# A decoder trunk with three kinds of heads: four VectorE edits and another order of projections, index scores and search

## The chip, the cores and the metric

The kernel runs on one core of one Trainium2 chip. The metric is the device time of one execution in microseconds (us), as the median of the runs.

## The reference, cut to what matters

One layer for 1024 positions of width 1024, all in float32: a combined input projection, three groups of heads, a SiLU gate, an output projection and norms.

```python
h = x
u = rms_norm(h, attn_norm)
proj = einsum('bsd,dc->bsc', u, w_in)
(dq, dk, dv, sq, ckv, iq, ik, iw, rq, rk, rv, gate) = split(proj)

# group A: differential attention, 6 heads of two softmaxes each, causal
p = softmax(where(causal, einsum('bqhcd,bkhcd->bhcqk', qb, k) * scale, NEG))
a = p[:, :, 0] - lam * p[:, :, 1]
o_a = rms_norm(einsum('bhqk,bkhd->bqhd', a, v), diff_norm) * (1 - lam_init)

# group B: DSA, 6 heads; an indexer of 8 heads picks 256 keys for each query
rel = relu(einsum('bqhd,bsd->bqhs', iqb, ik))
score = einsum('bqhs,bqh->bqs', rel, iwb) * IDX_SCALE
_, sel = top_k(where(causal, score, NEG), 256)
# softmax over the selected keys of the latent c_kv, then up-projection

# group C: 4 heads of chunkwise retention with rotary q and k

mixed = concatenate([o_a, o_b, o_c], -1)
y = silu(gate) * mixed
out = rms_norm(h + einsum('bsc,cd->bsd', y, w_out), final_norm)
```

## The kernel before

Every float32 product of a projection is made of three TensorE products of a high and a low part of the operands (`mm3`, L130 to L132: high by high, high by low, low by high). A projection *unit* (q0, k0, g0, iq2 and so on) is 128 columns of the input projection: two halves of 512 positions with 24 matmuls each, into a PSUM tile `pG`, of which there are two. Weights come by DMA and are split on GpSimd (L119, L123). The g units are the gate: their eviction `gate_evac` takes exp(-x), Ln(1 + .), exp(-.) on ScalarE (L818, L820, L821), copies x from PSUM on ScalarE (L113, called through `cp`) and multiplies on VectorE (L822).

The stages, in the order of the program:

- The norm of x and its transposition (`prep_a`, `prep_b`).
- The index scores (`idx_scores`): for each of 8 heads (two for each of the units iq0 to iq3) and the query blocks 7 to 2, matmuls into a score tile `pS` (L342, L343), a relu on ScalarE (L345) and a multiply-add on VectorE (L350). A projection unit's result goes to DRAM and comes back in another layout (`stack`, tiles `st`) before scores can use it. In this block the order on TensorE is the order of the program text (`manual_schedule`): `interleave` mixes streams, each piece of work that a stream yields having a cost, and a stream's weight saying what share of the time it gets.
- One big `interleave` of three streams: `diff` for three pairs of heads (weight `wd` 36), the top-k search `topk` (weight `wt` 13), and most remaining projection units (weight `wg` 119). Here a list scheduler fixes each engine's order when the program is built, on the costs it assumes.
- DSA for the first half of the queries beside retention and the first output projection, then the second half with the other output projections.

`diff` has 48 softmax pairs (6 heads by 8 query blocks). For each, TensorE makes two score tiles (L649, `pS`, two buffers), VectorE adds the mask and takes the row's extreme (L660, which frees the score tile), ScalarE takes the exponential and the row sum (L662), and then `comb`: two reciprocals (L674, L676), a scaling of the first softmax on GpSimd (L675), the lambda multiplication of a 128x1 column (L677) and a multiply-add (L678). TensorE then transposes (L609) and multiplies by v (L624).

`topk` finds for each query the 256th largest index score bit by bit: 31 bits, in each of which VectorE counts for three blocks (L377) and ScalarE for three (L391), followed by three tiny VectorE operations (L396, L397, L398). After the last bit, the *ties* (L418 to L428) turn scores and threshold into an additive mask `bias` for each of the blocks 7, 6, 5, 4, 3 and 2, which DSA needs: a sign on ScalarE and seven VectorE operations.

Of the kernel before, what the change touches and what calls it, by code (L numbers as in the profile page):

```python
# [2 lines left out]

# [1 line left out]

# [23 lines left out]
    0, 384, 768, 1152, 1536, 1664, 2176, 2248, 2504, 2760, 3016)  # L29
WA = 384 + 72  # L30
C_R = (C_RQ, C_RK, C_RV)
K = {'mk': 'up ky', 'mp': 's2 g5 g4', 'rt': ('hl', 'pq'), 's0': ('gg', 'gg', 'ag', 'gg', 'vg', 'gg', 'vg', 'vg'), 'xp': 2, 'bufs': (8, 3, 3, 5, 3, 4, 1), 'pp': (7,), 'rot': 0, 'order': 'g0 g1 k1 q1 k2', 'order2': 'q2 g2 rq g6 s0 ck g7 s1 M g3 rv rk | ', 'wd': 36, 'wt': 13, 'wg': 119, 'gw': 56, 'rw': 26, 'rx': 132, 'pw': 40, 'ow': 84, 'nf': 2, 'ev': 200, 'late': 8, 'de': ('aa', 'aa', 'aa'), 'da': 'ax', 'gd': (7, 4, 2), 'hlp': 'sqkk', 'tkp': '', 'vt': 'v', 'rs': 'x', 'nv': 1, 'dn': 'v', 'gy': 'a', 'gm': 'v', 'ws': 'gg', 'oe': ('av', 'gg'), 'one': 0, 'idx': (42, 40), 'iqs': 'iq2 iq3 q0 k0'}
NST, NP, NPQ, NW, NHL, NHALF, NY = K["bufs"]


# [22 lines left out]
def interleave(*streams):  # L58
    for _ in mix(*streams):
        pass  # L60
# [8 lines left out]
class Trunk:  # L69
# [238 lines left out]
    def stack(self, key, g, order, c0=0, c1=S):  # L308
        n, _, r, _ = self.qd[key].shape
        q = self.slot("st", [128, S], FR)  # L310
# [45 lines left out]
    def topk(self):  # L356
        nc = self.nc
        gd = K["gd"]
        ga = tuple(b for b in range(7, 1, -1) if b not in gd)
        nv = {b: 128 * (b + 1) for b in range(2, NB)}  # L360
        sc = self.sc
        jv = self.const("jv", [128, 1024], BF)
        ja = self.const("ja", [128, 1024], mybir.dt.int8)
        hb = self.const("hb", [128, 1024], BF)
        nc.gpsimd.tensor_scalar(hb, sc[7].bitcast(BF)[:, 1::2], 1.0, 0.0, op0=OP.mult, op1=OP.add)
        cols = {b: j for j, b in enumerate(gd + ga)}
        nd_, nc_ = len(gd), len(cols)
        thr = self.const("thr", [128, nc_])
        for b, j in cols.items():
            nc.vector.memset(thr[:, j:j + 1], nv[b] - TOPK + 0.5 if b in gd else float(nv[b] - 2 * TOPK + 1))  # L370
        c = self.const("tk_c", [128, nc_], I32)
        m = self.const("tk_m", [128, nc_], I32)
        cnt = self.const("tk_n", [128, nc_])

        def count(b, t, op, bit=0):
            j = cols[b]
            nc.vector.tensor_scalar(jv[:, :nv[b]], hb if b == 7 and bit >= 16 else sc[b], t, 0.0, op0=op, op1=OP.add,  # L377
                                    accum_out=cnt[:, j:j + 1])

        def cut(b):  # L380
            return c[:, cols[b]:cols[b] + 1].bitcast(F)

        for b in gd + ga:
            count(b, 0.0, OP.is_ge)
            yield 0.8
        nc.vector.tensor_scalar(m, cnt, float(TOPK), -1.0, op0=OP.is_lt, op1=OP.mult)
        nc.vector.tensor_scalar(c, m, 1 << 30, None, op0=OP.bitwise_xor)
        for bit in range(30, -1, -1):
# [12 lines left out]
        for b in ga:  # L401
            count(b, cut(b), OP.is_gt)
        cf = c[:, nd_:].bitcast(F)
        nc.vector.scalar_tensor_tensor(w[:, 0], cf, -1.0, cf, op0=OP.mult, op1=OP.max)
        nc.vector.tensor_scalar(w[:, 1], cnt[:, nd_:], float(TOPK), 2.0 ** -24 * (1 + 2.0 ** -10), op0=OP.is_ge,
                                op1=OP.mult)
        nc.vector.tensor_tensor(w[:, 0], w[:, 0], w[:, 1], OP.mult)
        nc.vector.tensor_tensor(cf, cf, w[:, 0], OP.add)
        yield 2.4
        A, C, T3 = (self.sct[b].bitcast(BF) for b in (7, 5, 3))  # L410
        self.bias = {0: self.cb[:, 896:], 1: self.cb[:, 768:], 7: A[:, :1024], 6: A[:, 1024:1920], 5: C[:, :768],
                     4: C[:, 768:1408], 2: C[:, 1408:1792], 3: T3[:, :512]}
        for b in (7, 6, 5, 4, 3, 2):
            n, T = nv[b], cut(b)
            bias = self.bias[b]
            sg, eq, pre = jv[:, :n], hb[:, :n], sc[b]
            nd = self.sb.tile([128, 1], F, name=self.name("nd"), tag="nd", bufs=2)
            nc.scalar.activation(sg, sc[b], AF.Sign, bias=T, scale=-1.0, accum_out=nd)  # L418
            (nc.gpsimd if "e" in K["tkp"] else nc.vector).tensor_scalar(eq, sg, 0.0, 1.0, op0=OP.is_equal, op1=OP.mult)
            nc.vector.tensor_tensor_scan(pre, eq, eq, 0.0, OP.add, OP.bypass)  # L420
            nc.vector.tensor_tensor(nd, nd, pre[:, n - 1:n], OP.add)
            nc.vector.tensor_scalar(nd, nd, 0.5, TOPK - n / 2.0, op0=OP.mult, op1=OP.add)
            nc.vector.scalar_tensor_tensor(eq, pre, nd, eq, op0=OP.is_gt, op1=OP.mult)
            nc.vector.tensor_tensor(eq, eq, sg, OP.max)
            if "a" in K["tkp"]:
                nc.scalar.activation(bias, eq, AF.Copy, scale=NEG)
            else:
                (nc.gpsimd if "b" in K["tkp"] else nc.vector).tensor_scalar(bias, eq, NEG, 0.0, op0=OP.mult, op1=OP.add)  # L428
            yield n / 1024 * 5

    def pair(self, tag, bufs):
# [198 lines left out]
    def diff(self, pair):  # L630
# [35 lines left out]
        def comb(v):  # L666
# [6 lines left out]
            else:  # L673
                nc.vector.reciprocal(mx[:, 2:3], mx[:, 2:3])  # L674
                nc.gpsimd.tensor_scalar(P[0], P[0], mx[:, 2:3], 1.0, op0=OP.mult, op1=OP.mult)  # L675
                nc.vector.reciprocal(mx[:, 3:4], mx[:, 3:4])  # L676
                nc.vector.tensor_tensor(mx[:, 3:4], mx[:, 3:4], self.nlam, OP.mult)  # L677
                nc.vector.scalar_tensor_tensor(P[1], P[1], mx[:, 3:4], P[0], op0=OP.mult, op1=OP.add)  # L678
            return P[1]

# [18 lines left out]
    def dsa(self, pair, half):  # L699
        nc = self.nc  # L700

        def head(a):
            e = half * 512 + 512
            return [self.stack(f"sq{pair}", a, "hl", e - 512, e)] + [self.stack(f"kk{pair}", a, o, 0, e)
                                                                     for o in ("hl", "lh")]

        def scores(st, i):
            q2, kh, kl = st
# [100 lines left out]
    def gate_evac(self, c):  # L809
        nc = self.nc  # L810
        if c < 6:
            self.gd[c] = self.dram(f"gd{c}", [128, S])
        d = self.gd[c]

        def evac(half, ps):
            t = self.sb.tile([128, 2, 512], F, name=self.name("gt"), tag="hl", bufs=NHL)
            e, y = t[:, 0], t[:, 1]
            nc.scalar.activation(e, ps, AF.Exp, scale=-1.0)  # L818
            self.cp(K["gy"], y, ps)
            nc.scalar.activation(e, e, AF.Ln, bias=1.0)  # L820
            nc.scalar.activation(e, e, AF.Exp, scale=-1.0)  # L821
            (nc.gpsimd if K["gm"] == "g" else nc.vector).tensor_tensor(y, y, e, OP.mult)  # L822
            nc.sync.dma_start(d[:, half * 512:half * 512 + 512], y)
        return evac

    def run(self):
# [148 lines left out]
```

## Time and profile before

| what | value |
|---|---|
| median of 3 runs (lowest, highest) | 783.7 us (782.78, 785.11) |
| the profiled execution, its span | 781.83 us, 780.1 us |
| granted TensorE clock, mean over the span | 0.983 |
| TensorE matmul, busy | 720.0 us, 92% |
| VectorE, busy | 562.0 us, 72% |
| ScalarE, busy | 452.6 us, 58% |
| GpSimd, busy | 314.5 us, 40% |

The span is what the trace covers; the execution's own time is 1.7 us longer. Busy times are sums over instructions of one profiled execution. Two instructions that follow each other on TensorE overlap in the trace, so its busy share is no measure of how close it is to its peak.

### The profile page before, as it was taken

How to read it: one execution, taken by the hardware profiler on the slowest of the kernel's cores; microseconds unless marked ns; L12 is line 12 of the kernel's file. 1: busy time of each engine (PE TensorE's matmuls, PEld its weight loads, DVE VectorE, ACT ScalarE, POOL GpSimd, SP SyncE). 2: the span in 40 equal slices, each digit the busy share in tenths (PEclk: the TensorE clock that was granted, in tenths of full speed). 3: DMA queues.
4: the chain of work that ended last, by engine and by line, in shares of the span. 5: the costliest groups of instructions: out<-in, count | busy, mean ns of one | idle time of the engine just before them, and what ended most of it. 6: DMA issues, size and time to landing. Idle time of an engine off the chain costs nothing.

```text
span 780.1 us, 12935 instructions
## 1 busy us (share of the span) xinstructions
PE 720.0 (92%) x4314; PEld 590.4 (76%) x4314; DVE 562.0 (72%) x1319; ACT 452.6 (58%) x1004; POOL 314.5 (40%) x343
## 2 busy tenths in 40 slices
PE   3899999999999999979998879998978999999996
PEld 3798888888877898756876667897856777787884
DVE  5920277789999999989999999425676776664443
ACT  4521255559788876887855756532465666554332
POOL 6402323324415358437656788325732432120000
PEclk9999999999999999989999999999998999999998
DMA  9303645454375263361276385346579864313351
GB/s 333 79 1 81 189 137 158 133 140 116 105 183 149 71 176 95 107 158 47 66 202 183 115 241 151 114 162 212 162 228 277 272 204 119 117 48 109 119 176 59
DMA packets 93250, 113.05 MB, mean 145 GB/s; under 512 B 11904, under 2 KB 63488, under 8 KB 93056
## 3 DMA queue, kind: packets, MB, share of 16 engines
q1 hardware_dynamic: 91888, 109.61, 48.8%
q10 hardware_dynamic: 1296, 2.62, 0.9%
q8 instruction: 34, 0.56, 0.3%
q14 instruction: 32, 0.26, 0.1%
HBM read 75.50 MB, written 36.18 MB: 143 GB/s over the span
## 4 chain that ended last, share of the span: by engine, by line
PE 56%; DVE 23%; DMA 9%; issue 5%; ACT 4%; POOL 2%; SPq 1%; DVEq 0%; ACTq 0%; POOLq 0%
PE pG L130 5%; PE pG L131 5%; PE pG L132 5%; PE pB L624 5%; PE pB L609 4%; PE pG L283 4%; PE pG L282 4%; PE pG L931 4%; PE pG L284 4%; PE pG L932 4%; PE pG L930 4%; DVE jv L377 3%; DVE pp L678 2%; PE pS L343 2%; DMA wr<-in_w_in_dram 2%
## 5 line engine op out<-in xcount | busy, mean ns | idle before, releaser
L130 PE MATMUL pG<-uh,wh 128*128 128x512 f32 x352 | 141.6, 402 | 0.8 <-DVE vt L117 0.5
L132 PE MATMUL pG<-uh,wl 128*128 128x512 f32 x352 | 139.5, 396 | 0.0
L131 PE MATMUL pG<-ul,wh 128*128 128x512 f32 x352 | 139.4, 396 | 0.0
L123 POOL TENSOR_TENSOR wl<-wr,wh 128x512 fp32r<-128x512 f32 x56 | 79.7, 1439 | 110.9 <-PE pG L131 58.7
L391 ACT ACTIVATE ja<-sc,tk_c 128x896 int8<-128x896 f32 (+2 forms) x93 | 83.3, 896 | 19.9 <-DVE tk_c L398 12.6
L113 ACT ACTIVATE pt<-pB 128x512 f32<-128x512 f32 (+2 forms) x120 | 58.6, 496 | 41.2 <-PE pB L609 41.1
L609 PE MATMUL pB<-ident,pp 128*128 128x128 f32 x432 | 72.7, 286 | 9.1 <-ACT pt L113 2.1
L130 PEld LDWEIGHTS pG<-uh,wh 128*128 128x128 f32 x352 | 66.4, 189 | 15.0 <-issue 1.3
L132 PEld LDWEIGHTS pG<-uh,wl 128*128 128x128 f32 x352 | 66.3, 188 | 14.9
L131 PEld LDWEIGHTS pG<-ul,wh 128*128 128x128 f32 x352 | 66.4, 188 | 13.6 <-issue 0.7
L609 PEld LDWEIGHTS pB<-ident,pp 128*128 128x128 f32 x432 | 50.4, 143 | 25.8 <-issue 8.9
L377 DVE TENSOR_SCALAR_CACHE_REDUCE jv<-sc,tk_c 128x640 bf16<-128x640 f32 (+4 forms) x81 | 69.1, 853 | 0.7
L624 PE MATMUL pB<-pt,v 128*64 128x128 f32 x864 | 66.1, 288 | 2.7 <-ACT pt L113 2.0
L675 POOL TENSOR_SCALAR pq<-pq,mx 128x896 f32<-128x896 f32 (+7 forms) x48 | 41.4, 864 | 61.3 <-DVE mx L674 48.5
L119 POOL TENSOR_SCALAR wh<-wr 128x512 fp32r<-128x512 f32 x56 | 41.5, 745 | 60.5 <-DMA wr<-in_w_in_dram 58.4
L624 PEld LDWEIGHTS pB<-pt,v 128*64 128x64 f32 x864 | 53.7, 140 | 15.0 <-issue 6.1
L649 PE MATMUL pS<-st,st 128*128 128x512 f32 (+3 forms) x144 | 44.8, 373 | 13.3 <-DVE mx L660 10.6
L283 PE MATMUL pG<-wl,uh 128*128 128x256 f32 x192 | 55.0, 287 | 2.1 <-POOL wl L123 2.1
L282 PE MATMUL pG<-wh,uh 128*128 128x256 f32 x192 | 54.7, 287 | 2.1 <-POOL wh L119 1.0
L345 ACT ACTIVATE pp<-pS 128x1024 f32<-128x1024 f32 (+5 forms) x48 | 36.5, 760 | 31.2 <-PE pS L343 31.1
L350 DVE SCALAR_TENSOR_TENSOR sc<-pp,iw,sc 128x1024 f32<-128x1024 f32 (+5 forms) x42 | 43.6, 1045 | 14.7 <-ACT pp L345 14.0
L284 PE MATMUL pG<-wh,ul 128*128 128x256 f32 x192 | 53.8, 282 | 0.0
(220 smaller groups left out, 1772.1 us busy)
## 6 DMA issues: line engine op xcount, KB each, us to landing
wr<-in_w_in_dram SPq DMA_DIRECT2D x56, 256.0 KB, 3.1
st<-qdq SPq DMA_DIRECT2D x24, 256.0 KB, 4.3
st<-qkk SPq DMA_DIRECT2D x18, 256.0 KB, 6.2
x<-in_x_dram SPq DMA_DIRECT2D x8, 512.0 KB, 6.6
qiq<-hl SPq DMA_DIRECT2D x16, 256.0 KB, 3.5
st<-qiq SPq DMA_DIRECT2D x8, 512.0 KB, 3.4
wr<-in_w_out_dram SPq DMA_DIRECT2D x16, 256.0 KB, 4.3
xr<-in_x_dram SPq DMA_DIRECT2D x8, 512.0 KB, 3.6
```

The lines of the kernel that those rows point to most:

```text
L113: self.nc.scalar.activation(out, in_, AF.Copy)
L123: (self.nc.vector if e2 == "v" else self.nc.gpsimd).tensor_tensor(lo, src, hi.bitcast(F), OP.subtract)
L130: mm(ps, wh, xh, start=start, stop=False)
L131: mm(ps, wh, xl, start=False, stop=False)
L132: mm(ps, wl, xh, start=False, stop=stop)
L282: mm(ps, uh, hs[k], start=k == 0, stop=False)
L283: mm(ps, uh, ls[k], start=False, stop=False)
L284: mm(ps, ul, hs[k], start=False, stop=k == KC - 1)
L377: nc.vector.tensor_scalar(jv[:, :nv[b]], hb if b == 7 and bit >= 16 else sc[b], t, 0.0, op0=op, op1=OP.add, accum_out=cnt[:, j:j + 1])
L391: nc.scalar.activation(ja[:, :nv[b]], sc[b], AF.Sign, bias=cut(b), scale=-1.0, accum_out=cnt[:, cols[b]:cols[b] + 1])
L609: nc.tensor.transpose(p[:, k], pr[:, (k0 + k) * 128:(k0 + k + 1) * 128], self.ident)
L624: self.last = nc.tensor.matmul(o[u * 64:(u + 1) * 64], vals[k], pts[g, a][:, k, u * 128:(u + 1) * 128], start=k == (i if u else 0), stop=k ...
```

## The change

Five edits.

1. In `comb` the lambda multiplication is a tensor_scalar with `nlam` as a scalar for each row, where it was a tensor_tensor of two 128x1 columns.
2. In `gate_evac` the copy of x from PSUM is left out, and the VectorE multiplication reads PSUM.
3. The ties are a generator of their own. They have six VectorE operations for a block where they had seven: the maximum is folded into the operation ahead of it (`> nd`, then plus the sign) and the last one compares with 0.5. Blocks 3 and 2 come right after the search, and 7, 6, 5 and 4 are a stream beside the first half of DSA. `jv` and `hb` become rotating buffers.
4. The table `K` has `'idx': (42, 30)` for (42, 40), `'iqs': 'iq2 iq3'` for 'iq2 iq3 q0 k0', and a new `'tk0': (18, 21)`: the units q0 and k0 leave the index block and are interleaved with the first 18 pieces of the search.
5. In the first half of DSA the two K tiles of a head share one `st` buffer.

```diff
-        jv = self.const("jv", [128, 1024], BF)
+        jv = self.sb.tile([128, 1024], BF, name="jv", tag="jv", bufs=1)
...
-                     4: C[:, 768:1408], 2: C[:, 1408:1792], 3: T3[:, :512]}
-        for b in (7, 6, 5, 4, 3, 2):
-            n, T = nv[b], cut(b)
-            bias = self.bias[b]
-            sg, eq, pre = jv[:, :n], hb[:, :n], sc[b]
+                     4: C[:, 768:1408], 3: T3[:, :512], 2: T3[:, 512:896]}
+        self.cut = cut
+
+    def ties(self, blocks):
+        nc = self.nc
+        for b in blocks:
+            n, T = 128 * (b + 1), self.cut(b)
+            sg = self.sb.tile([128, 1024], BF, name=self.name("sg"), tag="jv", bufs=1)[:, :n]
+            eq = self.sb.tile([128, 1024], BF, name=self.name("eq"), tag="hb", bufs=1)[:, :n]
+            pre = self.sc[b]
             nd = self.sb.tile([128, 1], F, name=self.name("nd"), tag="nd", bufs=2)
-            nc.scalar.activation(sg, sc[b], AF.Sign, bias=T, scale=-1.0, accum_out=nd)
-            (nc.gpsimd if "e" in K["tkp"] else nc.vector).tensor_scalar(eq, sg, 0.0, 1.0, op0=OP.is_equal, op1=OP.mult)
+            nc.scalar.activation(sg, pre, AF.Sign, bias=T, scale=-1.0, accum_out=nd)
+            nc.vector.tensor_scalar(eq, sg, 0.0, 1.0, op0=OP.is_equal, op1=OP.mult)
             nc.vector.tensor_tensor_scan(pre, eq, eq, 0.0, OP.add, OP.bypass)
-            nc.vector.tensor_tensor(nd, nd, pre[:, n - 1:n], OP.add)
-            nc.vector.tensor_scalar(nd, nd, 0.5, TOPK - n / 2.0, op0=OP.mult, op1=OP.add)
-            nc.vector.scalar_tensor_tensor(eq, pre, nd, eq, op0=OP.is_gt, op1=OP.mult)
-            nc.vector.tensor_tensor(eq, eq, sg, OP.max)
...
+            nc.vector.tensor_scalar(nd, nd, pre[:, n - 1:n], 0.5, op0=OP.add, op1=OP.mult)
+            nc.vector.tensor_scalar(nd, nd, TOPK - n / 2.0, None, op0=OP.add)
+            nc.vector.scalar_tensor_tensor(eq, pre, nd, sg, op0=OP.is_gt, op1=OP.add)
+            nc.vector.tensor_scalar(self.bias[b], eq, 0.5, NEG, op0=OP.is_gt, op1=OP.mult)
...
-                nc.vector.tensor_tensor(mx[:, 3:4], mx[:, 3:4], self.nlam, OP.mult)
+                nc.vector.tensor_scalar(mx[:, 3:4], mx[:, 3:4], self.nlam, None, op0=OP.mult)
...
+            kk = [None, None]
+            if not half:
+                t = self.slot("st", [128, 2, 512], FR)
+                kk = [t[:, j] for j in range(2)]
...
             nc.scalar.activation(e, ps, AF.Exp, scale=-1.0)
-            self.cp(K["gy"], y, ps)
             nc.scalar.activation(e, e, AF.Ln, bias=1.0)
             nc.scalar.activation(e, e, AF.Exp, scale=-1.0)
-            (nc.gpsimd if K["gm"] == "g" else nc.vector).tensor_tensor(y, y, e, OP.mult)
+            nc.vector.tensor_tensor(y, ps, e, OP.mult)
...
         self.setup_late()
+        tk = seq(self.topk(), self.ties((3, 2)))
+        interleave((islice(tk, K["tk0"][0]), K["tk0"][1]), (units("q0 k0"), 21))
         interleave((seq(*(self.diff(p) for p in range(3))), K["wd"]),
-                   (self.topk(), K["wt"]),
+                   (tk, K["wt"]),
                    (units(K["order"] + " " + K["order2"].split("|")[0]), K["wg"]))
         self.v_load()
-        interleave((seq(*(self.dsa(p, 0) for p in range(3))), 100),
+        interleave((seq(*(self.dsa(p, 0) for p in range(3))), 100), (self.ties((7, 6, 5, 4)), 110),
```

What the built order makes of it shows at three places. The first is TensorE at the end of the index scores. Before, the last two index matmuls are the rows 641 and 642 of TensorE, and the projection beside them (`pG_1321`) is the second half of k0:

```order
L132 MATMUL pG_1321<-uh,wl_1231 128x512
L342 MATMUL pS_1347<-kkh_296,st_1273 128x384
L343 MATMUL pS_1347<-kkl_297,st_1273 128x384
L130 MATMUL pG_1321<-uh,wh_1230 128x512
L131 MATMUL pG_1321<-ul,wh_1230 128x512
L132 MATMUL pG_1321<-uh,wl_1231 128x512
L130 MATMUL pG_1321<-uh,wh_1230 128x512
L131 MATMUL pG_1321<-ul,wh_1230 128x512
```

In the changed kernel they are the rows 732 and 733 (now L344 and L345), and the projection beside them is a late one of g1, of which `pG_1727` is the second half:

```order
L133 MATMUL pG_1727<-uh,wl_1604 128x512
L344 MATMUL pS_1212<-kkh_296,st_1174 128x512
L345 MATMUL pS_1212<-kkl_297,st_1174 128x512
L131 MATMUL pG_1727<-uh,wh_1603 128x512
L344 MATMUL pS_1219<-kkh_296,st_1174 128x384
L345 MATMUL pS_1219<-kkl_297,st_1174 128x384
L132 MATMUL pG_1727<-ul,wh_1603 128x512
L133 MATMUL pG_1727<-uh,wl_1604 128x512
```

So 91 more rows stand ahead of the last index score: the rest of k0, both halves of g0 and the larger part of g1.

The second place is TensorE at the first score of `diff`. Before it is row 709, L649:

```order
L130 MATMUL pG_1546<-uh,wh_1536 128x512
L131 MATMUL pG_1546<-ul,wh_1536 128x512
L132 MATMUL pG_1546<-uh,wl_1537 128x512
L649 MATMUL pS_1413<-st_1402,st_1399 128x512
L649 MATMUL pS_1413<-st_1402,st_1399 128x384
```

In the changed kernel it is row 765, now L652, behind a later unit:

```order
L133 MATMUL pG_1769<-uh,wl_1760 128x512
L131 MATMUL pG_1769<-uh,wh_1759 128x512
L132 MATMUL pG_1769<-ul,wh_1759 128x512
L652 MATMUL pS_1489<-st_1478,st_1475 128x512
L652 MATMUL pS_1489<-st_1478,st_1475 128x384
```

The number of rows ahead of it has grown by 56.

The third place is VectorE at the ties. Before, block 7 comes first (1024 columns) from row 646 on, among rows of `diff`; `hb` and `jv` are its scratch, `nd` its counts:

```order
L419 TENSOR_SCALAR hb<-jv 128x1024
L676 RECIPROCAL mx_3675<-mx_3675 128x1
L420 SCALAR_TENSOR_TENSOR sc_705<-hb 128x1024
L117 COPY vt_3934<-pG_3940 128x384
L677 TENSOR_TENSOR mx_3675<-mx_3675,nlam 128x1
L674 RECIPROCAL mx_3824<-mx_3824 128x1
L421 TENSOR_TENSOR nd_5625<-nd_5625,sc_705 128x1
L678 SCALAR_TENSOR_TENSOR pp_3679<-pp_3679,mx_3675,pq_3676 128x256
L422 TENSOR_SCALAR nd_5625<-nd_5625 128x1
L423 SCALAR_TENSOR_TENSOR hb<-sc_705,nd_5625,hb 128x1024
L424 TENSOR_TENSOR hb<-hb,jv 128x1024
L428 TENSOR_SCALAR sc_705<-hb 128x1024
```

In the changed kernel the ties begin with block 3 (512 columns) from row 686 on, and the lambda multiplication is now L680:

```order
L426 TENSOR_SCALAR eq_5610<-sg_5609 128x512
L680 TENSOR_SCALAR mx_4031<-mx_4031,nlam 128x1
L427 SCALAR_TENSOR_TENSOR sc_709<-eq_5610 128x512
L681 SCALAR_TENSOR_TENSOR pp_4035<-pp_4035,mx_4031,pq_4032 128x640
L428 TENSOR_SCALAR nd_5611<-nd_5611,sc_709 128x1
L679 RECIPROCAL mx_4086<-mx_4086 128x1
L677 RECIPROCAL mx_4198<-mx_4198 128x1
L429 TENSOR_SCALAR nd_5611<-nd_5611 128x1
L680 TENSOR_SCALAR mx_4086<-mx_4086,nlam 128x1
L430 SCALAR_TENSOR_TENSOR eq_5610<-sc_709,nd_5611,sg_5609 128x512
L681 SCALAR_TENSOR_TENSOR pp_4090<-pp_4090,mx_4086,pq_4087 128x768
L431 TENSOR_SCALAR sc_709<-eq_5610 128x512
```

The tensor_tensor on L424 has no counterpart, and the lambda row has become a tensor_scalar. Block 7 follows at row 710 and the last block, 4, ends at row 784; before, the last one ended at row 776. The first score tile of DSA is reduced behind all of these rows in both orders.

## Rows read from the trace of the kernel before

**Rows 1.** The page, busy times, and VectorE in 40 slices of the span.

```profile
PE 720.0 (92%) x4314; PEld 590.4 (76%) x4314; DVE 562.0 (72%) x1319; ACT 452.6 (58%) x1004; POOL 314.5 (40%) x343
...
DVE  5920277789999999989999999425676776664443
```

**Rows 2.** Windows: stretch, length, busy time and instructions of each engine.

```profile
core 0: us, PE busy (x) PEld busy (x) DVE busy (x) ACT busy (x) POOL busy (x), PEclk, DMA share, GB/s
...
200.00:300.00 100.00, 97.51 (x642) 82.53 (x642) 95.38 (x275) 82.27 (x192) 44.28 (x58) 1.00 0.52 135
300.00:400.00 100.00, 90.70 (x490) 70.71 (x490) 95.66 (x244) 79.08 (x182) 60.97 (x63) 0.97 0.38 102
...
450.00:500.00 50.00, 44.70 (x283) 36.32 (x282) 42.13 (x84) 29.62 (x70) 37.85 (x36) 1.00 0.63 177
```

**Rows 3.** Waits, 160 (VectorE 165) to 470 us: sum in us, times, longest.

```profile
PE pS L649 <- DVE mx L660: 10.6, 9, 3.0
...
DVE tk_n L396 <- ACT ja L391: 4.5, 4, 2.1
```

**Rows 4.** Pieces of the chain that ended last, 400 to 620 us: start, us, what.

```profile
449.69 1.08 DVE hb L424
...
451.04 0.90 DVE mx L677
```

**Rows 5.** Timeline of TensorE: start us, us, instruction.

```profile
160.46 0.34 PE L343 MATMUL pS<-kkl,st 128*128 128x384 f32 x1
...
161.10 0.40 PE L132 MATMUL pG<-uh,wl 128*128 128x512 f32 x1
...
163.44 0.40 PE L130 MATMUL pG<-uh,wh 128*128 128x512 f32 x1
...
176.04 0.40 PE L649 MATMUL pS<-st,st 128*128 128x512 f32 x1
```

**Rows 6.** Timeline of VectorE: first and last multiply-add of `diff`.

```profile
185.20 1.15 DVE L678 SCALAR_TENSOR_TENSOR pp<-pp,mx,pq 128x896 f32<-128x896 f32 x1
...
508.82 0.48 DVE L678 SCALAR_TENSOR_TENSOR pp<-pp,mx,pq 128x256 f32<-128x256 f32 x1
```

**Rows 7.** VectorE instructions by line, whole span: count, busy us, mean ns, idle before.

```profile
L377 DVE TENSOR_SCALAR_CACHE_REDUCE jv<-sc,tk_c 128x640 bf16<-128x640 f32 (+4 forms) x81 | 69.1, 853 | 0.7
...
L677 DVE TENSOR_TENSOR mx<-mx,nlam 128x1 f32<-128x1 f32 x48 | 17.8, 370 | 0.4
...
L123 DVE TENSOR_TENSOR hl<-pG,hl 128x512 fp32r<-128x512 f32 x20 | 13.7, 683 | 15.0 <-ACT hl L113 14.9
...
L822 DVE TENSOR_TENSOR gt<-gt 128x512 f32<-128x512 f32 x16 | 13.6, 847 | 1.1 <-ACT gt L821 1.0
...
L424 DVE TENSOR_TENSOR hb<-hb,jv 128x1024 bf16<-128x1024 bf16 (+5 forms) x6 | 4.8, 802 | 0.0
```

**Rows 8.** Single lines: shortest/median/longest in ns, first and last start.

```profile
L677 DVE TENSOR_TENSOR mx<-mx,nlam x48: 133/156/1281, 184.8 to 508.6; 128x1 f32<-128x1 f32 x48
...
L422 DVE TENSOR_SCALAR nd<-nd x6: 128/140/154, 408.9 to 467.6; 128x1 f32<-128x1 f32 x6
...
L397 DVE TENSOR_SCALAR tk_m<-tk_n x31: 146/173/1261, 173.4 to 396.4; 128x6 int32<-128x6 f32 x31
```

**Rows 9.** Timeline of GpSimd and VectorE at one long lambda row.

```profile
261.99 2.53 POOL L123 TENSOR_TENSOR wl<-wr,wh 128x512 fp32r<-128x512 f32 x2 [1.67 <-PE pG L131]
...
263.25 1.28 DVE L677 TENSOR_TENSOR mx<-mx,nlam 128x1 f32<-128x1 f32 x1
```

**Rows 10.** Timeline at one gate tile: ScalarE, TensorE (its wait in brackets), VectorE.

```profile
264.74 0.59 ACT L818 ACTIVATE gt<-pG 128x512 f32<-128x512 f32 x1
...
265.21 0.60 ACT L113 ACTIVATE gt<-pG 128x512 f32<-128x512 f32 x1
...
265.86 0.39 PE L282 MATMUL pG<-wh,uh 128*128 128x256 f32 x1 [0.71 <-ACT gt L113]
...
271.82 0.68 DVE L822 TENSOR_TENSOR gt<-gt 128x512 f32<-128x512 f32 x1
```

More of the change, by code (lines that the diff above doesn't have):

```diff
@@ L2 @@
 from contextlib import ExitStack
+from itertools import islice
 import numpy as np
@@ L31 @@
 C_R = (C_RQ, C_RK, C_RV)
-K = {'mk': 'up ky', 'mp': 's2 g5 g4', 'rt': ('hl', 'pq'), 's0': ('gg', 'gg', 'ag', 'gg', 'vg', 'gg', 'vg', 'vg'), 'xp': 2, 'bufs': (8, 3, 3, 5, 3, 4, 1), 'pp': (7,), 'rot': 0, 'order': 'g0 g1 k1 q1 k2', 'order2': 'q2 g2 rq g6 s0 ck g7 s1 M g3 rv rk | ', 'wd': 36, 'wt': 13, 'wg': 119, 'gw': 56, 'rw': 26, 'rx': 132, 'pw': 40, 'ow': 84, 'nf': 2, 'ev': 200, 'late': 8, 'de': ('aa', 'aa', 'aa'), 'da': 'ax', 'gd': (7, 4, 2), 'hlp': 'sqkk', 'tkp': '', 'vt': 'v', 'rs': 'x', 'nv': 1, 'dn': 'v', 'gy': 'a', 'gm': 'v', 'ws': 'gg', 'oe': ('av', 'gg'), 'one': 0, 'idx': (42, 40), 'iqs': 'iq2 iq3 q0 k0'}
+K = {'mk': 'up ky', 'mp': 's2 g5 g4', 'rt': ('hl', 'pq'), 's0': ('gg', 'gg', 'ag', 'gg', 'vg', 'gg', 'vg', 'vg'), 'xp': 2, 'bufs': (8, 3, 3, 5, 3, 4, 1), 'pp': (7,), 'rot': 0, 'order': 'g0 g1 k1 q1 k2', 'order2': 'q2 g2 rq g6 s0 ck g7 s1 M g3 rv rk | ', 'wd': 36, 'wt': 13, 'wg': 119, 'gw': 56, 'rw': 26, 'rx': 132, 'pw': 40, 'ow': 84, 'nf': 2, 'ev': 200, 'late': 8, 'de': ('aa', 'aa', 'aa'), 'da': 'ax', 'gd': (7, 4, 2), 'hlp': 'sqkk', 'tkp': '', 'vt': 'v', 'rs': 'x', 'nv': 1, 'dn': 'v', 'ws': 'gg', 'oe': ('av', 'gg'), 'one': 0, 'idx': (42, 30), 'iqs': 'iq2 iq3', 'tk0': (18, 21)}
 NST, NP, NPQ, NW, NHL, NHALF, NY = K["bufs"]
@@ L306, in to_dram, with stack @@
         return evac
-    def stack(self, key, g, order, c0=0, c1=S):
+    def stack(self, key, g, order, c0=0, c1=S, q=None):
         n, _, r, _ = self.qd[key].shape
-        q = self.slot("st", [128, S], FR)
+        if q is None:
+            q = self.slot("st", [128, S], FR)
         d = self.qd[key][g]
@@ L361, in topk @@
         sc = self.sc
-        jv = self.const("jv", [128, 1024], BF)
+        jv = self.sb.tile([128, 1024], BF, name="jv", tag="jv", bufs=1)
         ja = self.const("ja", [128, 1024], mybir.dt.int8)
-        hb = self.const("hb", [128, 1024], BF)
+        hb = self.sb.tile([128, 1024], BF, name="hb", tag="hb", bufs=1)
         nc.gpsimd.tensor_scalar(hb, sc[7].bitcast(BF)[:, 1::2], 1.0, 0.0, op0=OP.mult, op1=OP.add)
@@ L411, in topk @@
         self.bias = {0: self.cb[:, 896:], 1: self.cb[:, 768:], 7: A[:, :1024], 6: A[:, 1024:1920], 5: C[:, :768],
-                     4: C[:, 768:1408], 2: C[:, 1408:1792], 3: T3[:, :512]}
-        for b in (7, 6, 5, 4, 3, 2):
-            n, T = nv[b], cut(b)
-            bias = self.bias[b]
-            sg, eq, pre = jv[:, :n], hb[:, :n], sc[b]
+                     4: C[:, 768:1408], 3: T3[:, :512], 2: T3[:, 512:896]}
[7 more added lines that the diff above has]
+            pre = self.sc[b]
             nd = self.sb.tile([128, 1], F, name=self.name("nd"), tag="nd", bufs=2)
-            nc.scalar.activation(sg, sc[b], AF.Sign, bias=T, scale=-1.0, accum_out=nd)
-            (nc.gpsimd if "e" in K["tkp"] else nc.vector).tensor_scalar(eq, sg, 0.0, 1.0, op0=OP.is_equal, op1=OP.mult)
+            nc.scalar.activation(sg, pre, AF.Sign, bias=T, scale=-1.0, accum_out=nd)
+            nc.vector.tensor_scalar(eq, sg, 0.0, 1.0, op0=OP.is_equal, op1=OP.mult)
             nc.vector.tensor_tensor_scan(pre, eq, eq, 0.0, OP.add, OP.bypass)
-            nc.vector.tensor_tensor(nd, nd, pre[:, n - 1:n], OP.add)
-            nc.vector.tensor_scalar(nd, nd, 0.5, TOPK - n / 2.0, op0=OP.mult, op1=OP.add)
-            nc.vector.scalar_tensor_tensor(eq, pre, nd, eq, op0=OP.is_gt, op1=OP.mult)
-            nc.vector.tensor_tensor(eq, eq, sg, OP.max)
[L425 to L428, printed above, removed]
+            nc.vector.tensor_scalar(nd, nd, pre[:, n - 1:n], 0.5, op0=OP.add, op1=OP.mult)
+            nc.vector.tensor_scalar(nd, nd, TOPK - n / 2.0, None, op0=OP.add)
+            nc.vector.scalar_tensor_tensor(eq, pre, nd, sg, op0=OP.is_gt, op1=OP.add)
+            nc.vector.tensor_scalar(self.bias[b], eq, 0.5, NEG, op0=OP.is_gt, op1=OP.mult)
             yield n / 1024 * 5
@@ L703, in head @@
             e = half * 512 + 512
-            return [self.stack(f"sq{pair}", a, "hl", e - 512, e)] + [self.stack(f"kk{pair}", a, o, 0, e)
-                                                                     for o in ("hl", "lh")]
+            kk = [None, None]
+            if not half:
+                t = self.slot("st", [128, 2, 512], FR)
+                kk = [t[:, j] for j in range(2)]
+            return [self.stack(f"sq{pair}", a, "hl", e - 512, e)] + [self.stack(f"kk{pair}", a, o, 0, e, k)
+                                                                     for o, k in zip(("hl", "lh"), kk)]
         def scores(st, i):
```

## The prediction

> **What bounds the kernel now.** I read the page first for the busy shares of the engines and for the slices of the span. TensorE is busy 92% of the span and VectorE 72% [rows 1], which alone would say that VectorE doesn't matter. The slices say otherwise: VectorE stands at nine tenths from the 9th slice to the 23rd, and at six or below over most of the rest. The stage behind that is the one in which the differential attention, the top-k search and the projections run side by side. In windows of that stage VectorE is busy 95.4 and 95.7 us of 100, and TensorE has gaps (90.7 of 100 in the second one); from 450 to 500 us VectorE has room again, 42.1 of 50 [rows 2]. The waits say who waits for whom: the scores of `diff` (L649) wait 10.6 us for VectorE's reduction (L660), which is late with giving back a score buffer, and VectorE itself waits almost for nothing, 4.5 us being its largest sum [rows 3]. So in this stage VectorE is the bound. The chain that ended last agrees: between 400 and 470 us it goes through the tie operations and through the one-column lambda multiplication (L677) [rows 4]. Outside of the stage TensorE is the bound: ahead of it TensorE issues without gaps, one 512-column matmul each 0.234 us (161.10 to 163.44 is ten steps) [rows 5].
>
> The sum below is therefore made for the stretch from the first multiply-add of `diff` (185.20) to the last (508.82) [rows 6], 323.6 us, with what moves its start added. It is made against the profiled execution, 781.83 us; the median of the runs, 783.7, lies 1.9 above, and I add that at the end. A measurement of this kernel can tell about 0.3% (2.4 us) from no change: faster is below 781.3, slower above 786.1.
>
> **Step 1, the new order on TensorE: the stage starts later.** The new text asks for q0 and k0 beside the first bits of the search, but the rows of the order show something else. The last index score is row 642 before and row 733 after, since g0 and most of g1 now stand ahead of index heads 6 and 7. These are 91 rows at 0.234: the index scores end 21.3 us later than 160.46. The first score of `diff` moves from row 709 to row 765, 56 rows: 13.1 us later than 176.04 [rows 5]. The projection work that stands ahead is gone from the later stage, but there TensorE isn't the bound. So the start term is **+13.1**, and it becomes +21.3 if the search, which needs all index scores, is what everything then waits for. Nothing hides this term: VectorE has little to do while TensorE is still projecting.
>
> **Step 2, VectorE's rows in the stretch.** (a) The lambda multiplication costs 17.8 us in 48 rows, mean 370 ns [rows 7], but its median is 156 and its longest 1281 [rows 8]. A look at a long one: it begins at 263.25 and takes 1.28 us, and a GpSimd subtraction that began earlier ends at 264.52, 0.01 us ahead of it [rows 9]. Of the 48 rows, 15 are longer than 200 ns, and each of them ends within 20 ns of the end of a GpSimd instruction. It is a wait for GpSimd, not work; the reciprocals beside it, with one tensor, never show it. The new form has one tensor and a per-row scalar. The nearest row is the one-column tensor_scalar of the ties (L422): 128 to 154 ns, none long [rows 8], though 5 of its 6 rows ran wholly inside a GpSimd instruction. So I take 156 ns: 47 rows in the stretch by 0.214 us, **-10.1**; bounds -10.1 and 0. (b) The ties lose the maximum (L424), 4.8 us in 6 rows [rows 7]: **-4.8**. The other tie rows keep form and number, and I cost them at nothing. (c) The gate multiplication now reads PSUM and one SBUF tensor. Today it takes 847 ns [rows 7], and the subtraction L123 that reads PSUM and SBUF at the same size takes 683 [rows 7]. 14 rows stand in the stretch before, 12 after (two more now stand ahead of it): 14 by 0.847 less 12 by 0.683, **-3.7**. The 16 copies on ScalarE go as well; ScalarE has room, so they count nothing. (d) One L123 row moves ahead of the stretch, **-0.7**. Against that one bit more of the search falls into the stretch, with one of the first counts: 4 rows of 0.853 (L377) [rows 7] and three small ones of about 0.17 as L397's median [rows 8], **+3.9**. The sum of step 2 is -15.4.
>
> [...]
>
> **Step 3, the tail.** From 450 to 500 us VectorE is idle 7.9 us of 50 [rows 2], while TensorE still projects. The change has moved 13.1 us of projections ahead, so some of that idle time goes: bounds 0 and -7.9; I take **-3.0**, below half, since TensorE too has only 5.3 us free there.
>
> **Step 4, what is left over.** By the order 12 more 512-column steps stand behind the last score of `diff` than before, 2.8 us at 0.234; behind 509 us TensorE has gaps to take some: bounds 0 and +2.8, I take **+1.0**. The shared slot of the two K tiles in the first DSA half frees buffers that no wait of before asks for: 0.
>
> Sum: +13.1 - 15.4 - 3.0 + 1.0 = -4.3, or 777.5 for the profiled execution and **779.5** as the median.
>
> **Rivals.** *B, a larger gain.* The tail's whole 7.9 goes and nothing is left over: 4.9 + 1.0 more, 773.6. For it: the waits of TensorE for VectorE, 10.6 us [rows 3], could shrink besides, which leads to 767. Against it: the late start eats most of what VectorE saves.
>
> *C, the wait stays, or passes to the next instruction.* Behind 4 of the 15 long lambda rows stands at once the multiply-add L678, which also has two SBUF tensors; if GpSimd is still busy, L678 waits in its place. These four are 2.7 us of the saving; without them the time is 782.2. If the new form itself waits, the whole 10.1 is gone: 789.6. For it: the tensor_scalar L397, six columns, has rows up to 1261 ns [rows 8]; against it, L422 with one column. [...]
>
> *D, the gate's PSUM buffer (ends on the other side).* The copy L113 released the projection's PSUM tile; now it is held until the multiplication, which stands behind three ScalarE steps and in VectorE's full queue. At 264.74 the first exponential reads the tile, the copy ends at 265.81, and the next user on TensorE (L282) already waits 0.71 us for that copy; the multiplication ends only at 272.50 [rows 10]. There are two such buffers and TensorE works in order, so behind that matmul the scores of `diff` would wait too, which feed VectorE. The price of this place is 272.50 - 265.81, 6.7 us: 786.2; a second such place would make it some 792. For it: this row. Against it: TensorE is ahead of VectorE, so a wait there may be swallowed, and the order may have the multiplication earlier. It decides from about 4 us of such waits that reach VectorE.
>
> *E, the search is the longest.* Its first bit waits for the last index score, 21.3 later instead of 13.1. Then +8.2: 787.7. For it: the ties stand at the end of the stage and DSA needs them. Against it: search and `diff` share VectorE, and whichever is late, the other fills in.
>
> The change also doesn't do all that it says: the ties of blocks 7 to 4 were to run beside the first DSA half, but in the order all of them still stand ahead of it.
>
> **How the numbers follow.** The forecast (775 to 782): 0.38, of which 0.33 is below 781.3. B: 0.19. C: 0.18, two thirds of it within 0.3%. D: 0.16, of which 0.11 is above 786.1. E: 0.09, 0.07 above. So faster 0.52, same 0.24, slower 0.24. The range reaches from B's low end, 767, to between the two ends of D, 790.
>
> **What would show it.** The first score of `diff` at about 189 us and the last index score at about 182 (step 1). The lambda row at a mean of 0.15 to 0.16 us, and L678 in sum no longer than before (2a, C). The gate row at 0.68 us from PSUM (2c); on TensorE no waits for it on the projection tile (D). The last multiply-add of `diff` at about 504 to 506. Wrong would be: TensorE's waits on the projection tile growing by several us; VectorE's share in 200 to 400 falling below nine tenths, which would say that something else became the bound; or a first bit of the search that sets the end.

## The result and the profile after

The changed kernel takes 790.21 us (median; 788.8 to 794.86), the kernel before 784.73 us in the same comparison: ratio 1.0097, 95% interval 1.0069 to 1.0125. It is slower by 1%, and the forecast was 0.5% faster. The profiled execution took 792.64 us, 10.8 more than the one of before, so terms read from these two traces add up to 10.8 and not to the 5.5 between the medians.

The page of the changed kernel, busy times and VectorE's slices, against [rows 1]:

```profile
PE 724.3 (92%) x4314; PEld 592.4 (75%) x4314; DVE 549.3 (69%) x1313; ACT 444.7 (56%) x988; POOL 311.3 (39%) x343
...
DVE  5921285548999999999897999416567676564443
```

VectorE did lose work, 562.0 to 549.3 us, and the run of nines starts one slice later. The windows, first the columns, then the stretches of [rows 2], then the stretch from the first multiply-add of `diff` to the end of the last:

```profile
core 0: us, PE busy (x) PEld busy (x) DVE busy (x) ACT busy (x) POOL busy (x), PEclk, DMA share, GB/s
...
200.00:300.00 100.00, 96.87 (x638) 82.66 (x638) 98.34 (x285) 82.67 (x192) 46.43 (x58) 1.00 0.50 129
...
300.00:400.00 100.00, 88.41 (x467) 66.12 (x468) 95.08 (x235) 78.81 (x181) 55.54 (x57) 0.97 0.35 92
...
450.00:500.00 50.00, 42.51 (x211) 32.38 (x212) 46.32 (x99) 31.74 (x76) 38.50 (x33) 0.90 0.63 172
...
202.10:516.60 314.50, 288.69 (x1721) 231.83 (x1720) 289.08 (x755) 234.23 (x545) 178.66 (x186) 0.97 0.49 132
```

The same stretch of the kernel before:

```profile
185.20:509.30 324.10, 300.05 (x1798) 243.02 (x1798) 299.52 (x751) 241.10 (x558) 183.58 (x190) 0.98 0.49 133
```

The stretch is 9.6 us shorter, and VectorE's busy time in it 10.4 us less (299.5 to 289.1): its idle time is the same, 24.6 and 25.4. But it starts 16.9 us later. TensorE's busy time in it fell as well, by 11.4 us (300.1 to 288.7), with 77 matmuls fewer. The timelines of TensorE (last index score, first score of `diff`) and of VectorE (first and last multiply-add, now L681), against [rows 5, 6]:

```profile
184.58 0.34 PE L345 MATMUL pS<-kkl,st 128*128 128x384 f32 x1
...
191.96 0.57 PE L652 MATMUL pS<-st,st 128*128 128x512 f32 x2
...
202.05 2.11 DVE L681 SCALAR_TENSOR_TENSOR pp<-pp,mx,pq 128x896 f32<-128x896 f32 x1
...
516.16 0.48 DVE L681 SCALAR_TENSOR_TENSOR pp<-pp,mx,pq 128x256 f32<-128x256 f32 x1
```

So the sum of the two traces is +16.9 up to the first multiply-add, -9.6 to the end of the last, +3.5 behind it (270.8 to 274.3 us): +10.8. Of the first term, 13.1 are the 56 rows of the order at the price of the prediction; another 2.5 are waits that the index block of before doesn't have. The waits of TensorE from 88 to 192 us:

```profile
PE pS L344 <- DMA st<-qiq: 1.6, 2, 0.8
...
PE pS L344 <- ACT pp L347: 0.6, 1, 0.6
...
PE pG L131 <- DVE hl L124: 0.3, 1, 0.3
```

The first of them is for the layouts of the index queries (`st<-qiq`). That these now have less projection work to hide behind is my reading; no run shows it. The VectorE rows of the change, against [rows 7, 8]; the second fence is the multiply-add of before:

```profile
L681 DVE SCALAR_TENSOR_TENSOR pp<-pp,mx,pq 128x896 f32<-128x896 f32 (+7 forms) x48 | 50.5, 1052 | 4.7 <-POOL pq L678 4.2
...
L680 DVE TENSOR_SCALAR mx<-mx,nlam 128x1 f32<-128x1 f32 x48 | 9.9, 207 | 0.3
...
L828 DVE TENSOR_TENSOR gt<-pG,gt 128x512 f32<-128x512 f32 x16 | 10.9, 681 | 6.2 <-ACT gt L827 6.2
...
L680 DVE TENSOR_SCALAR mx<-mx,nlam x48: 182/209/217, 201.1 to 515.8; 128x1 f32<-128x1 f32 x48
```

```profile
L678 DVE SCALAR_TENSOR_TENSOR pp<-pp,mx,pq 128x896 f32<-128x896 f32 (+7 forms) x48 | 48.3, 1006 | 1.9 <-POOL pq L675 0.8
```

No lambda row is long any more, as expected, but each takes 0.21 us and not the 0.156 that I took, the middle of the old rows [rows 8], and the multiply-add behind it got 2.2 us longer in sum. The gate row is 0.68 us from PSUM. TensorE has no wait for the gate's tile anywhere in this trace.

### The profile page after: what moved, and what is told of

Read it like the earlier page. It is cut to its first block, busy times and chain, and to the rows that moved or that the text cites. A ratio compares the mean times of both kernels' runs of the same rounds, so it can differ in the third digit from the quotient of the medians.

```text
span 790.9 us, 12929 instructions
## 1 busy us (share of the span) xinstructions
PE 724.3 (92%) x4314; PEld 592.4 (75%) x4314; DVE 549.3 (69%) x1313; ACT 444.7 (56%) x988; POOL 311.3 (39%) x343
## 4 chain that ended last, share of the span: by engine, by line
PE 54%; DVE 22%; DMA 10%; issue 6%; ACT 4%; POOL 2%; SPq 2%; DVEq 0%; ACTq 0%; POOLq 0%
DVE jv L379 5%; PE pG L131 5%; PE pG L132 5%; PE pG L133 5%; PE pB L627 5%; PE pB L612 4%; PE pG L939 4%; PE pG L940 4%; PE pG L938 4%; PE pG L284 3%; PE pG L283 3%; PE pG L285 3%; DVE pp L681 2%; DMA wr<-in_w_in_dram 2%; DVE pq L663 2%
## 5 line engine op out<-in xcount | busy, mean ns | idle before, releaser
L132 PE MATMUL pG<-ul,wh 128*128 128x512 f32 x352 | 141.2, 401 | 0.0
L124 POOL TENSOR_TENSOR wl<-wr,wh 128x512 fp32r<-128x512 f32 x56 | 76.8, 1389 | 113.2 <-PE pG L132 74.0
L120 POOL TENSOR_SCALAR wh<-wr 128x512 fp32r<-128x512 f32 x56 | 38.4, 689 | 64.9 <-DMA wr<-in_w_in_dram 55.9
L652 PE MATMUL pS<-st,st 128*128 128x512 f32 (+3 forms) x144 | 45.4, 382 | 14.7 <-DVE mx L663 9.7
```

The source lines that it names most:

```text
L124: (self.nc.vector if e2 == "v" else self.nc.gpsimd).tensor_tensor(lo, src, hi.bitcast(F), OP.subtract)
L132: mm(ps, wh, xl, start=False, stop=False)
```

## The experiments

All ratios are to the kernel before in the same batch, with 95% intervals.

**The order edit apart from the others.** The first kernel has all edits but the fourth:

```diff
-'idx': (42, 30), 'iqs': 'iq2 iq3', 'tk0': (18, 21)
+'idx': (42, 40), 'iqs': 'iq2 iq3 q0 k0'
-        interleave((islice(tk, K["tk0"][0]), K["tk0"][1]), (units("q0 k0"), 21))
```

> All edits but the fourth: index scores stand beside iq2, iq3, q0 and k0 again, and the search begins with diff, as in the kernel before. Theory 1 (the later start costs what the VectorE edits save): the last index score is back at about 161 us and the first score of diff at 176, the stretch between first and last multiply-add of diff stays near 314 us as in the changed kernel, so the last one ends near 500 and the kernel takes 775 to 780 us, 0.6 to 1.2% below before. Rival 2 (an edit inside the stage or behind it costs, by waits for the gate's PSUM tile or the late ties): it stays at 787 to 791 us. Rival 3 (the stage isn't bound by VectorE, its length just follows from where TensorE has work): within 0.3% of before.

Measured: 783.85 us, ratio 1.000 (0.9972 to 1.0028). The second has the fourth edit alone, the reverse of that diff on the kernel before:

> The kernel before with the fourth edit alone: index weights 42 and 30 beside iq2 and iq3 only, q0 and k0 beside the first 18 pieces of the search. By the order the last index score is TensorE row 733 and the first score of diff row 765, as in the changed kernel. Theory 1: the first score of diff at about 192 us, the last multiply-add 10 to 17 us later than before, 794 to 801 us in all, 1.2 to 2.1% slower than before. Rival 2: within 0.5% of before. Rival 3: 5 to 6 us slower, as the changed kernel.

Measured: 801.3 us, 1.0236 (1.0198 to 1.0273). So the order edit is what makes the change slower; alone it costs far more than within the change. But the other edits, which take 11.1 us off the late order (801.3 to 790.2), take nothing off the old one. The windows of the stretch, edits alone and order alone:

```profile
183.80:509.30 325.50, 300.46 (x1779) 246.02 (x1778) 292.64 (x741) 236.40 (x544) 182.56 (x191) 0.96 0.48 134
```

```profile
202.80:530.10 327.30, 296.65 (x1781) 242.72 (x1780) 305.80 (x758) 241.20 (x560) 181.01 (x186) 0.96 0.47 128
```

With the edits alone VectorE has 6.9 us less work than before (292.6) in a stretch of the same length (325.5): it is idle instead. TensorE's busy time is the same, 300.5, though for 19 matmuls fewer, at a granted clock of 0.96 where it was 0.98. These are single executions: the one profiled here took 787.0 us, 3.2 above the median of its kernel, and that of before 781.8, some 2.7 below. So the medians say that the edits gain nothing here, and the traces do not say in which stretch.

**Single edits.** Lambda alone (the one line of edit 1), ties alone (edit 3) and the gate alone (edit 2):

> The kernel before with the lambda multiplication as tensor_scalar alone. Theory 1: the row takes 0.21 us as in the changed kernel instead of 0.37, L678 gets some 2 us of the wait in sum, VectorE loses 5 to 6 us of work in the stretch and the kernel gains as much: 778 to 781 us, 0.4 to 0.8% faster. Rival 2 or 3: within 0.3% of before.

Measured: 785.35 us, 1.0023 (0.9996 to 1.0051).

> The kernel before with the third edit alone: ties with six VectorE operations, blocks 3 and 2 first and the others as a stream of their own. Theory 1: VectorE loses 4 us in the stretch, the ties stand on the chain that ended last, so 780 to 783 us. Rival 2, where the new place of the ties costs: the scan of block 7 later than 404.6 us by the time of blocks 3 and 2, and DSA later with it, 786 to 789 us.

Measured: 787.34 us, 1.0046 (1.0022 to 1.0069).

> The kernel before with the gate edit alone: the copy from PSUM left out, the multiplication reading PSUM. Theory A: the multiplication at 0.68 us instead of 0.85, no waits of TensorE for the gate's tile, time within 0.4% of before. The rival that I forecast as D, TensorE waiting for the tile: 4 to 7 us slower, with waits of TensorE's projection matmuls for the multiplication.

Measured: 794.11 us, 1.0115 (1.0088 to 1.0143). Here the waits of rival D are in the trace, small ones; waits of TensorE from 170 to 520 us (L821 is the multiplication):

```profile
PE pS L649 <- DMA st<-qdk: 5.1, 3, 2.6
...
PE pG L130 <- DVE gt L821: 2.7, 4, 1.0
...
PE pG L282 <- DVE gt L821: 0.7, 1, 0.7
```

3.4 us of waits can't make 9.6, nor can three edits at +0.2, +0.5 and +1.2% make 0.0% together by adding up. Something else came with each of them. The next runs ask whether it was the order.

**Controls: another order of the same work.** One stream weight is changed; the list scheduler then builds another order. Of the 1219 VectorE instructions of the built program, 387 stand elsewhere in the sequence in the first control and 507 in the second. In the first control every instruction is as before; in the second and third the scheduler also gives two and one small copies (`yo<-pB`, 128x128) to ScalarE instead of VectorE.

```diff
-'wg': 119
+'wg': 122
```

> A control: the kernel before with one stream weight changed from 119 to 122 and no instruction changed; the scheduler puts many of them in another order. If the effect of a single edit can be read from a run of that edit alone, this stays within 0.3% of before. If the order that each build falls into is worth as much as the edits, it differs by 0.4 to 1% in either direction, 777 to 792 us, and single edits in the old order (lambda +0.2%, ties +0.5%, gate +1.2%) can't be put down to the edit itself.

Measured: 788.64 us, 1.0045 (1.0017 to 1.0073).

> A second control: the kernel before with the weight of diff at 38 instead of 36, no instruction changed. As for the first control: within 0.3% if orders are equal in worth, 0.4 to 1% off in either direction if not.

Measured: 790.52 us, 1.0074 (1.0048 to 1.0101).

> A third control: the kernel before with the weight of diff at 34 instead of 36, no instruction changed. Theory, that the order of before is a picked one and any other order costs about 4 to 6 us: 786 to 792 us, as the other two controls. Rival, orders scatter to both sides: as likely below 784.

Measured: 792.33 us, 1.0111 (1.0072 to 1.015). Each of the three loses, on average 0.8% or 6 us. The clock, the third figure from the end of a window's row, is lower there too; the control at 38, then before:

```profile
300.00:400.00 100.00, 88.73 (x456) 68.84 (x455) 96.55 (x225) 77.60 (x177) 60.39 (x63) 0.93 0.34 95
...
400.00:500.00 100.00, 90.28 (x455) 68.54 (x455) 93.14 (x192) 58.29 (x137) 67.26 (x59) 0.90 0.60 172
```

```profile
400.00:500.00 100.00, 87.74 (x511) 68.49 (x508) 90.08 (x182) 60.56 (x139) 71.35 (x62) 0.98 0.61 174
```

The granted TensorE clock is 0.93 and 0.90 of full speed in these two stretches, where before has 0.97 [rows 2] and 0.98. Over all executions its mean was 0.980 to 0.983 in each batch of the kernel before, and 0.970 to 0.978 in every experiment here but one. In the trace of before it stands at 1.00 or at 0.50: five stretches of 3.4 to 6.8 us, 26 us of the 780.1 in all, have 0.50. By these two levels, an estimate for the other executions, a mean of 0.97 is 6% of the span at the lower one, and 0.98 is 4%. Among the 29 executions of before in the first batch, one with a clock lower by 0.01 took 5 us longer (a fitted line, correlation -0.79). The line isn't a firm price: the other four batches of before give 1.2 to 6.0 us, and the largest of them, 32 executions, a correlation of only -0.28. Nor does a lower clock always come with a longer time: the edits alone, at a mean clock of 0.973, take as long as before. In the trace of before four of the five stretches begin at most 0.8 us from the end of a wait of TensorE of 2.1, 3.0, 1.9 and 1.8 us, the fifth behind its last matmul. The wait of 3.0 us is for a score buffer, and the window from 410 to 420 us around it has a clock of 0.83 (the third figure from the end):

```profile
416.71 1.22 PE L649 MATMUL pS<-st,st 128*128 128x512 f32 x2 [3.02 <-DVE mx L660]
...
410.00:420.00 10.00, 6.98 (x40) 5.02 (x39) 9.10 (x16) 5.35 (x11) 7.47 (x6) 0.83 0.59 182
```

Not every wait goes with a lower clock: the windows around one of 1.5 us at 318 us and one of 1.8 us at 462 us have 1.00. That an order with longer waits costs twice, by the waits and by the clock, wasn't shown. How much of the 6 us is the clock stays open; what a kernel would take at an unchanged clock wasn't tried.

The same on the changed kernel:

> The changed kernel with the weight of diff at 38 instead of 36, no instruction changed. Theory, that the changed kernel's order is one of many and not a picked one: within 5 us of 790 to either side, with no reason to be slower. Rival, every move away from these weights costs: 794 to 796 us.

Measured: 793.54 us, 1.0137 (1.0091 to 1.0184).

> The changed kernel with the weight of the projections at 122 instead of 119. Theory and rival as for the weight of diff: 785 to 795 to either side, or 794 to 796.

Measured: 794.42 us, 1.0138 (1.0096 to 1.018). Both a little slower than the changed kernel's 1.0097, with intervals that overlap.

**The square at another weight.** With the weight of `diff` at 38 none of the four orders is the one of before.

> All edits but the fourth, with the weight of diff at 38: with the control of before at 38 (+0.74%), the changed kernel at 38 (+1.37%) and the order edit at 38 this makes the same square of four kernels as at 36. Theory, that the edits save about 6 us of VectorE's time in any order and that the order of before at 36 is a favourable one: 0.74 - 0.77, about 0.0% against before, 780 to 788 us. Rival, the edits save nothing: +0.7%, as the control.

Measured: 787.87 us, 1.0055 (1.003 to 1.0081).

> The kernel before with the fourth edit alone and the weight of diff at 38. Theory: the later start costs 12 to 14 us on top of the control at 38, so 2.2 to 2.6% against before, 800 to 804 us. Rival, half of the order edit's 2.4% at 36 was the loss of a favourable order, and the loss comes but once: 1.0 to 1.7%.

Measured: 800.34 us, 1.0205 (1.0168 to 1.0242). Both squares, in per cent against the kernel before at 36:

| | old order | order edit | the order edit adds |
|---|---|---|---|
| weight 36, old VectorE code | 0 | +2.36 | 2.36 |
| weight 36, edits 1, 2, 3 and 5 | 0.00 | +0.97 | 0.97 |
| weight 38, old VectorE code | +0.74 | +2.05 | 1.31 |
| weight 38, edits 1, 2, 3 and 5 | +0.55 | +1.37 | 0.82 |

The order edit costs 0.8 to 2.4%, on average 1.4% or 10.7 us. The VectorE edits give 0.0 and 1.39% at 36, 0.19 and 0.68% at 38, on average 0.57% or 4.4 us. The clock is a rival for the zero at 36: by the first batch's line the edits' lower clock there, 0.973 for 0.981, would be some 4 us, an estimate. But at 38 the two kernels of the old order both have 0.974, and the edits give only 0.19%, so the clock can't be all of it.

**Is VectorE alone the bound?** TensorE's work is cut in the stage, in `gemm`:

```diff
+                    if c0 in (C_DQ + 128, C_DK + 256, C_DQ + 256):
+                        mm(ps, hs[k], uh, start=k == 0, stop=False)
+                        mm(ps, ls[k], uh, start=False, stop=k == KC - 1)
...
```

> The kernel before, with the product of the low part of u by the high part of the weights left out in the units q1, k2 and q2 (48 matmuls of 512 columns, 11.2 us at 0.234 us, all in the stage of diff and the search; the result loses that part of its precision). Theory A, in the order of before TensorE and VectorE bound that stage together: taking work from one alone gives little, 0 to 4 us, 780 to 784 us. Rival B, VectorE alone bounds it: no change. Rival C, TensorE alone, every us of its own work counts: 773 us, 11 less.

Measured: 785.09 us, 1.0018 (0.9998 to 1.0038).

> All edits but the fourth (the order of before), with the same 48 matmuls left out. Theory A, both bound the stage: now both have less, and the time falls by 8 to 11 us from the 784 that the edits alone took, to 773 to 776. Rival B, VectorE alone: as the edits alone, 784. Rival C, TensorE alone: 773, but then the run without the VectorE edits falls as far.

Measured: 779.52 us, 0.9925 (0.9899 to 0.9951). 11.2 us less of TensorE's work alone gives nothing against before, the VectorE edits alone nothing, both together 5 us. That is theory A's pattern at half its size; against the controls (+0.8%) the three would be about 5, 6 and 12 us faster, nearly a plain sum, so which of the two engines binds more isn't settled. Against before, a microsecond of neither engine is a microsecond of the kernel; against the controls VectorE's comes near it (6 us for 6.9 of work), and TensorE's to less than half (5 for 11.2).

**The output weights.** Behind `diff`, in the first DSA half, ScalarE waits 8.6 us for output weights to land in the kernel with the edits alone (509 to 625 us), VectorE 5.7 us for ScalarE's part of their split, and TensorE, in one place, 3.5 us for VectorE. That the last follows from the first two is what this split was to try.

```diff
-'oe': ('av', 'gg')
+'oe': ('gg', 'gg')
```

> All edits but the fourth, with all splits of the output weights on GpSimd instead of every second one on ScalarE and VectorE. Theory: behind diff both in-order engines stop at output weights that have not landed, TensorE waits for them in the first DSA half and loses clock, and what the lighter VectorE gains ahead is given back there; then this version is 4 to 8 us faster than the edits alone, 776 to 780, with less TensorE slack between 550 and 600 us. Rival: the slack there comes from the transfers themselves, then no change or slower, since GpSimd takes longer for a split.

Measured: 779.02 us, 0.9918 (0.9888 to 0.9947), the one other kernel with a mean clock of 0.982. Next the edits without the gate edit, first with the old split and then with the new one, and last the changed kernel with the new split:

> Lambda, ties and the shared slot in the order of before, the gate's copy kept. Theory: the gate edit costs in itself, since its PSUM tile is held until the multiplication (alone it was 9 us slower), so this is 4 to 9 us faster than all edits but the fourth (784), 775 to 780. Rival: the cost of the gate edit alone was that of another order, then within 0.4% of 784.

Measured: 784.19 us, 0.9991 (0.9961 to 1.0021), as with the gate edit (783.85): in this order the gate edit costs nothing, so its 1.2% alone wasn't its own.

> The same with all splits of the output weights on GpSimd. From all edits but the fourth this split took 4.8 us off. Theory: it does the same here, 771 to 776, or 779 if the run above is at 784.

Measured: 784.61 us, 1.000 (0.997 to 1.0029).

> The changed kernel with all splits of the output weights on GpSimd; by the order built, nothing ahead of the first DSA half moves. Theory: TensorE's waits in the first DSA half shrink as they did with all edits but the fourth, 785 to 787 us. Rival, that gain was one of another order behind it, as the version without the gate edit showed none: 788 to 792.

Measured: 790.47 us, 1.0083 (1.0042 to 1.0123). The split gives nothing in two of three kernels. The version at 779 us beats both kernels. In the traces it and the edits alone have the same order on TensorE for the first 2982 matmuls; from there to the end it takes 216.1 us, the edits alone 221.0 and the other four kernels of this comparison 219.4 to 221.8. So most of its gain comes in the part that it orders anew, and isn't shown to be the split's.

## Why the prediction was wrong

By the two traces the forecast is off by 15.1 us (+10.8 for -4.3): 3.8 in the start, 8.8 in the stretch (-9.6, where steps 2 and 3 together had -18.4) and 2.5 behind it. Of the 8.8, 5.0 are work that VectorE kept and 3.8 idle time that didn't go.

**Step 1, the later start (+13.1): right in kind, too small in the trace (+16.9).** The last index score came at 184.6 (forecast about 182) and the first score of `diff` at 192.0 (forecast about 189), late by the 2.5 us of waits, 1.6 of them for the index layouts, for which I had no term. Among the four pairs of the squares the order edit costs 10.7 us on average.

**Step 2, VectorE's rows (-15.4): the step that failed.** It was wrong twice. As work it was 10.4 us in the trace: the lambda row takes 0.21 us and not 0.156, which makes 7.9 us over its 48 rows (17.8 to 9.9) and not 10.3, and the multiply-add behind it takes 2.2 us more. That this is the lambda row's wait passed on (rival C) isn't shown: with the lambda edit alone the multiply-add takes 48.4 us in sum, where it had 48.3 before. And the work was then counted as time one for one, because VectorE was busy 95% and waited for almost nothing. The squares say 4.4 us on average, and in the old order 6.9 us less of VectorE's work gave nothing against before (6 us if the controls are the measure). In the changed kernel's trace the stretch did shrink by nearly what VectorE lost, but there TensorE had lost 11.4 us too, most of it moved ahead by the order edit. TensorE, at 97.5 of 100 us in the first of the windows [rows 2], had by its busy time hardly any more room than VectorE; I read its gaps in the second window as proof that it wasn't the bound, and took no account of the first. That both engines bind the stage fits these runs and the pair with less work for TensorE; the order and the clock, which change with each edit, keep it from being shown.

**No step at all for the order.** The kernel before has an order that the three controls lose 0.45 to 1.1% from, by a change of one weight. Every edit here leaves it. This would explain why each edit alone looks neutral or harmful, and it would lie within the 5.5 us too; how much of the changed kernel's loss it is depends on which of its own orders one compares, so I give no number.

**Step 3, the tail (-3.0): wrong.** The window from 450 to 500 us has 3.7 us of idle time left of 7.9, but the stage lies later in it, and TensorE's granted clock there was 0.90 where it had been 1.00 [rows 2]; over the whole stretch VectorE is idle as long as before (25.4 and 24.6 us). **Step 4, what is left over (+1.0): too small,** 3.5 in the trace.

**The rivals.** B didn't happen. Of C, the new form never waited; what passed to the multiply-add is open. D's mechanism exists (3.4 us of waits with the gate edit alone) but not in the changed kernel's trace. E forecast 787.7 by a late search, and the last of the search's rows did start 24.9 us later (L398 at 396.7 us before, now L400 at 421.6); but the last multiply-add was only 7.3 us later, so the late search was filled in with `diff`, as its counter-argument said. No run tested it alone. That the ties of blocks 7 to 4 stay ahead of DSA was right.

The gate's multiplication takes 681 ns from PSUM (667 to 692) and took 686 ns from SBUF, the middle of its 16 rows. So it was not made faster by PSUM, as my comparison of 683 with 847 [rows 7] had it: the 847 is a mean with six rows of 0.88 to 1.65 us in it, each of them ending 0.53 to 0.55 us behind a GpSimd instruction that ran when it began. What the edit saves, 2.7 us (13.6 to 10.9), are those waits.

Three readings of the prediction were off without bearing on the miss: VectorE's nines run from the 10th slice to the 25th, with one eight; the sum gives 779.4; and the four rows of rival C (275, 1281, 458 and 780 ns) lie 2.2 us above 156 ns, not 2.7.

## What to carry to other kernels

Ask of an engine that is busy 95% which other engine is at 95% beside it: a saving on one of the two may be worth far less than its size, here 4.4 us on average for 10.4 us of work in the trace. Where a scheduler lists the program anew on each edit, run a control that changes a weight and no instruction before believing any effect of 1%; here all three neighbours of the kernel before were slower, as one would expect of weights that had been picked. And work moved ahead of a stage can delay its start by more than it shortens the stage: here 56 matmuls went ahead of the work that VectorE was waiting to begin, its first multiply-add came 16.9 us later, and the stretch got 9.6 us shorter.

## What the runs showed of the hardware

A one-column tensor_scalar with a per-row scalar took 0.21 us, one with constants 0.14 [rows 8]. The first never waited for GpSimd, in 48 rows of 0.182 to 0.217 us, while the one-column tensor_tensor did in 15 of 48, with up to 1.281 us [rows 8]. A float32 multiplication of 128x512 took the same from PSUM and SBUF (0.681 us) as from SBUF twice (0.686) where it didn't wait for GpSimd, which it did in 6 of the 16 rows from SBUF. The granted clock, a mean of 0.970 to 0.983 over the span, was lower in three slower kernels with almost the same instructions in another order (0.972, 0.974 and 0.976, beside 0.980, 0.980 and 0.983 of before), and goes with the scatter of one kernel's executions, loosely (correlations of -0.17 to -0.79 in five batches).
